# A hybrid decoder layer on one core: the value products move behind the next half's key products, and attention runs three blocks ahead instead of four

## The chip, the core and the metric

The kernel runs on one core of a Trainium2 chip. A core has five engines, each with its own instruction stream: TensorE (PE; its weight loads are shown as PEld), VectorE (DVE), ScalarE (ACT), GpSimd (POOL) and SyncE (SP, which issues most DMAs). They wait for each other through semaphores. The metric is the device time of one execution in microseconds; the figure to predict is the median of several runs.

## The reference, cut to what matters

One layer of a decoder: a normalised input is projected once, and the columns go to a gated short convolution, to sliding-window attention (8 query heads on 2 key heads, a learned sink per head) and to cross-attention of 4 heads into 256 memory tokens. The three outputs are gated, joined and projected.

```python
def _layer(...):
    h = _rmsnorm(x, g_pre)
    z = h @ w_in
    cb, cc, ch, cg, q, k, v, ag, mq, mg = _split_cols(z)
    ...
    out_a = jax.nn.silu(cg) * cb * conv
    ...
    o_b = _window_prompt(q, k, v, sink_g)          # banded, 128-query blocks
    out_b = jax.nn.silu(ag) * o_b
    o_c = _mem_attend(mq.reshape(n, t, MEM_HEADS, HEAD_DIM), mem_k, mem_v)
    out_c = jax.nn.silu(mg) * o_c
    y = jnp.concatenate([out_a, out_b, out_c], axis=-1) @ w_out
    return x + _rmsnorm(y, g_post), new_conv, new_k, new_v
```

The prompt has 4096 positions, and a sample part has 8 sequences of 8 new tokens with caches of their own. All is float32.

## The kernel before

The first 933 us are the input projection (seven products in place of eight on blocks of 520 positions, each product as three passes over a high and a low part). The change does not touch it. What follows is one loop over 32 output blocks of 128 positions, and a block for the sample tokens; in it the output projection and the attention of later blocks run through each other on TensorE.

**An output block** (class Block): its gated input, mix, is split into a high part (mh, ScalarE, line 1559) and a low part (ml, VectorE, line 1560; it reads mix and mh). Then 48 products y of 128x512 follow (line 1578): two halves p of the columns, eight steps k each, three passes a step. Ahead of a step (p, k), whatever stands in `starts` for it is called. So n = 16 b + 8 p + k counts the steps of all blocks, and an entry at (0, 4) or (1, 4) puts attention work between the y products there. Two PSUM banks (pool z) are for y.

**A half** h is the attention of one block of 128 queries: chunk c = h // 2 holds 256 positions, i = h % 2. It is done in two steps.

- first_half(h): `window_scores` (tiles ws, in two bank pairs w, of which there are two). Keys stand in a form in which each score is one product over all 128 rows and one over 64 rows (the low part of a key); two of the 64-row products lie side by side in the array, and are placed by `tile_position`. They run whole, half, half, whole. Then `memory_transposes` of the half before (xt, in bank pair x, of which there is one; two copies take it out, one on VectorE, the next on ScalarE, line 1345), and `window_probabilities`: ScalarE and VectorE mask, find the maximum, take exponentials (line 1265) and normalise (sm).
- second_half(h): `memory_scores` (xs, bank pair x, line 1332), for two heads of the chunk's 256 queries, then its maximum (xmx), exponentials (xp, line 1159) and the shares (xrd, line 1160), by which GpSimd multiplies xp (line 1168). `products` of the half before: the memory values (`both_values`, line 1057: column halves of 64, two at once), the window values over all keys (line 1218, column halves), and the quarters (line 1224: 64 rows by 64 columns, four at once). Where a new chunk begins, two transposes of its values (line 1643). Then `window_turns`: eight transposes of sm (wt, line 1353), which ScalarE copies out (wpt, line 1283), and from which GpSimd makes two masked tiles each (affine selects: wpv, line 1288, and wpt in place, line 1291). Last `gates`: VectorE multiplies the values into mix.

In the steady part, block b calls first_half(b + 4) at its step (0, 4) and second_half(b + 4) at (1, 4). The values of h - 1 belong to second_half(h). The first halves, 2 to 6, start by the table EARLY within blocks 0 to 2. The split of block b + 1 stands at the start of block b.

TensorE runs in the order in which the program records its work until block 26. The order on the other engines is chosen by a planner from what each instruction needs. GpSimd also issues the loads of keys (kst, line 1086) and queries (q, line 1099); its queue is in order like the others'. The sample tokens' attention is cut into stages (`sample_mem`, `sample_window`) that are called four times a block from block 26 on.

## Time and profile before

| | us |
|---|---|
| median of 3 runs (1539.02 to 1540.51) | 1540.0 |
| the profiled execution | 1536.39 |
| its span, first to last instruction | 1534.7 |
| first y product | 933.2 |
| a steady block (18 of them in 327.04 us) | 18.17 |
| first y product of block 25 | 1404.8 |

The profile comes from a single execution. It lists each engine's busy time, who ended an engine's wait, a chain of waits followed back from the last instruction, and timelines. An instruction's name such as `xt<-ident,xp` says which tile it writes and from which it reads. An entry of TensorE counts the passes: an ordinary float32 product stands twice, a transpose or a rounded float32 product once. A matmul's end is modelled, so the difference from one start to the next is its price, and not its own length.

### The profile page before, as it was taken

Reading aid. Unit: us, or ns where it says so; the run is one execution under the profiler, and the core shown is the slowest. Engines: PE = TensorE matmul, PEld = TensorE weight load, DVE = VectorE, ACT = ScalarE, POOL = GpSimd, SP = SyncE. Lnnn points to the kernel's source line nnn. Section 1 sums busy time; section 2 is a strip of 40 time slices with the busy share of each in tenths; the row PEclk is TensorE's granted clock in tenths of the full one; section 3 lists DMA queues with packets and bytes.
Section 4 is the critical chain, followed back from the end, with each engine's and each line's share of the span. In section 5 each row is a group of like instructions: output and inputs, shape, how many; then the busy total and the mean of one; then the engine's idle time right before and its main releaser. Section 6 shows DMA issues by size and latency. Waiting matters only on the chain.

```text
span 1534.7 us, 30061 instructions
## 1 busy us (share of the span) xinstructions
PE 1516.2 (99%) x11341; PEld 1387.8 (90%) x11341; DVE 1151.6 (75%) x1965; ACT 797.7 (52%) x1949; POOL 393.1 (26%) x635
## 2 busy tenths in 40 slices
PE   9999999999999999999999999999999999999998
PEld 9999999999999999999999998777888888887776
DVE  5779887899988777896776768776767677776643
ACT  6776665576322222444454547665555556655532
POOL 0223323211400000000100303644455454444310
PEclk9999999999999999999999999999999999999999
DMA  9989999978855333578776789977877778877432
GB/s 255 166 252 223 286 285 261 277 237 295 207 181 180 126 126 119 197 235 284 233 270 230 221 293 270 245 156 152 161 149 148 148 149 163 157 158 148 135 109 96
DMA packets 178453, 306.28 MB, mean 200 GB/s; under 512 B 34437, under 2 KB 108165, under 8 KB 178277
## 3 DMA queue, kind: packets, MB, share of 16 engines
q1 hardware_dynamic: 130901, 227.38, 48.4%
q0 software_dynamic: 46688, 75.93, 25.4%
q8 instruction: 90, 1.47, 0.4%
q10 hardware_dynamic: 720, 1.05, 0.2%
q14 instruction: 54, 0.44, 0.1%
HBM read 197.23 MB, written 108.05 MB: 199 GB/s over the span
## 4 chain that ended last, share of the span: by engine, by line
PE 68%; DMA 13%; DVE 9%; issue 5%; ACT 2%; POOL 1%; SPq 1%; ACTq 0%; DVEq 0%; POOLq 0%
PE c L368 33%; PE y L1578 21%; PE ws L1309 3%; PE wo L1057 2%; DMA place<-in_xt 2%; PE wt L1353 2%; PE xs L1332 2%; PE xt L1341 1%; PE wo L1218 1%; DMA nat<-in_x_p 1%; DVE z L375 1%; PE wo L1224 1%; DMA wr_3A<-in_w_in 1%; DMA zs<-qd 1%; DMA md<-th 1%
## 5 line engine op out<-in xcount | busy, mean ns | idle before, releaser
L1578 PE MATMUL y<-wo,mh 128*128 128x512 f32 (+1 forms) x1040 | 336.0, 393 | 0.0
L375 DVE TENSOR_TENSOR z<-c,z 128x520 f32<-128x520 f32 (+1 forms) x308 | 194.1, 644 | 80.8 <-PE c L368 79.4
L1578 PEld LDWEIGHTS y<-wo,mh 128*128 128x128 f32 x1040 | 194.4, 188 | 39.7 <-issue 2.0
L1578 PE MATMUL y<-wo,ml 128*128 128x512 f32 (+1 forms) x520 | 201.3, 387 | 0.0
L1578 PEld LDWEIGHTS y<-wo,ml 128*128 128x128 f32 x520 | 98.0, 188 | 17.5
L1168 POOL TENSOR_SCALAR xp<-xp,xrd 128x256 f32<-128x256 f32 x128 | 60.5, 481 | 197.4 <-DVE xrd L1160 197.3
L1265 ACT ACTIVATE sm<-sm,wnm 128x128 f32<-128x128 f32 x256 | 99.4, 389 | 14.2 <-DVE wnm L1259 11.6
L1159 ACT ACTIVATE xp<-xs,xnm 128x256 f32<-128x256 f32 x128 | 59.5, 470 | 89.6 <-DVE xnm L1157 86.9
L1585 DVE TENSOR_TENSOR yn<-y,gpost 128x512 f32<-128x512 f32 (+1 forms) x66 | 45.3, 686 | 62.6 <-PE y L1578 61.7
L1099 POOL DMA_DIRECT2D q<-qd x96 | 60.2, 635 | 116.9 <-DVE wo L186 56.7
L1319 DVE COPY_PREDICATED sm<-wmask,ws 128x512 f32<-128x512 uint8 x60 | 43.9, 735 | 49.3 <-ACT sm L1318 49.2
L1291 POOL TENSOR_SCALAR_AFFINE_SELECT wpt<-wpt 128x512 f32<-128x512 f32 x64 | 64.9, 1033 | 43.4 <-ACT wpt L1283 43.1
L737 POOL CAST wmask<-negs 128x256 uint8<-128x256 f32 x1 | 0.7, 686 | 266.3 <-DMA negs<-in_wmask 266.3
L1318 ACT COPY sm<-ws 128x512 f32<-128x512 f32 x60 | 35.1, 586 | 65.0 <-PE ws L1309 65.0
L1309 PEld LDWEIGHTS ws<-kst,q 128*128 128x128 f32 (+1 forms) x480 | 50.3, 187 | 12.0 <-PE y L1578 0.9
L1309 PE MATMUL ws<-kst,q 128*128 128x256 f32 (+1 forms) x480 | 59.5, 299 | 0.8 <-PE y L1578 0.5
L276 ACT ACTIVATE nat<-nat 104x1024 f32<-104x1024 f32 x40 | 42.3, 1058 | 26.0 <-DMA nat<-in_x_p 26.0
L407 ACT CAST zh<-z 128x520 fp32r<-128x520 f32 x56 | 33.3, 624 | 35.0 <-DVE z L375 31.9
L377 ACT COPY z<-c 128x520 f32<-128x520 f32 (+1 forms) x44 | 24.4, 554 | 49.6 <-PE c L368 46.5
L1086 POOL DMA_DIRECT2D kst<-qd x64 | 38.7, 617 | 42.9 <-issue 24.5
L1586 ACT ACTIVATE y<-y 128x512 f32<-128x512 f32 (+1 forms) x66 | 37.9, 575 | 21.5 <-DVE yn L1585 21.4
L1265 ACT ACTIVATION_READ_ACCUMULATOR sm<-sm,wnm 128x1 f32 x256 | 47.8, 187 | 0.0
(976 smaller groups left out, 5088.9 us busy)
## 6 DMA issues: line engine op xcount, KB each, us to landing
q<-qd POOLq DMA_DIRECT2D x96, 256.0 KB, 6.9
xr<-in_x_p SPq DMA_DIRECT2D x32, 512.0 KB
nat<-in_x_p SPq DMA_DIRECT2D x39, 416.0 KB
o_yp<-xr SPq DMA_DIRECT2D x31, 512.0 KB
md<-th POOLq DMA_DIRECT2D x48, 260.0 KB, 6.2
qd<-zh SPq DMA_DIRECT2D x48, 260.0 KB
qd<-z SPq DMA_DIRECT2D x48, 260.0 KB
kst<-qd POOLq DMA_DIRECT2D x60, 192.0 KB, 3.8
```

What stands on the lines that cost most here:

```text
L276: S.activation(t[:RG], t[:RG], AF.Square, accum_out=r[:RG, i : i + 1])
L368: TE.matmul(bank[:, :HW], l, r, start=first and i == 0, stop=last and i == 3 * KH - 1)
L375: add = lambda dst, other: V.tensor_tensor(dst, c, other, op=ALU.add)
L1099: G.dma_start(self.q[64 * half : 64 * half + 64, i : i + 4, :].rearrange("p (j v) n -> p j v n", v=2), heads(part, j, self.ts))
L1159: S.activation(p[:, i, :], s[:, i, :], AF.Exp, bias=nm[:, i : i + 1], scale=SCALE, accum_out=den[:, i : i + 1])
L1168: G.tensor_scalar(p[:, i, :], p[:, i, :], self.rds[h][:, i : i + 1], 0.5, op0=ALU.mult, op1=ALU.mult)
L1265: S.activation(sm[:, hh, :], sm[:, hh, :], AF.Exp, bias=nm[:, hh : hh + 1], scale=SCALE, accum_out=den[:, hh : hh + 1])
L1291: G.affine_select(p3, p3, pattern=[[0, 4], [1, P]], compare_op=ALU.is_ge, fill=0.0, base=0, channel_multiplier=-1)
L1309: TE.matmul(out(kvh, col, bank), q(kvh, col, bank)[r], k(kvh, part)[r], start=first, stop=True, skip_group_check=not first, **place)
L1319: V.copy_predicated(sm4, third["wmask"].unsqueeze(1).to_broadcast([P, 2, 2, P]), s4[:, :, :, 0:P])
L1578: TE.matmul(acc, self.hl[l][:, k], wo[k][c0 // 512][:, r, c0 % 512 : c0 % 512 + c1 - c0], start=j == 0, stop=j == passes * KT - 1)
L1585: V.tensor_tensor(yn[:m, c0:c1], acc[:m], gpost[:m, c0:c1], op=ALU.mult)
```

## The change

- `products` leaves second_half and goes to first_half, behind `window_scores`. `memory_transposes` of the half before now opens first_half, ahead of `window_scores`. second_half keeps `memory_scores` and `window_turns`.
- `window_scores` runs its whole-row products for both key heads first, then the 64-row ones. `products` runs the quarters first (in its own copy of the code of `band_values`), then the column halves over all rows, then the memory values. They are written to bank pair x, no longer to w.
- `memory_scores(i)` takes all four heads for the 128 queries of one block, instead of two heads for 256 queries. Maximum, exponentials and shares are three functions now, called for both pairs of heads in turn. The memory values are computed for two pairs of heads of 128 columns each.
- In the steady part, block b calls first_half(b + 3) at (0, 4) and second_half(b + 3) at (1, 4). The halves up to 7 start by the tables first_at and second_at, spread over blocks 0 to 4. The sample stages come three or four quarters later.
- `gates` follows `window_probabilities` in the steady part, and precedes it while the halves start early.

```diff
@@ cross_softmax, in three @@
-        def cross_softmax(self, h, s, now=True):
+        def cross_maximum(self, h, s):
...
+        def cross_exps(self, h, s, nm):
...
+        def cross_shares(self, h, p=None):
+            nb, den = CT // P, self.rds[h]
+            rd = self.rds[h] = tiny.tile([P, 4], F32, tag="rd", name=f"xrd{self.c}_{h}")
             V.reciprocal(rd[:, :nb], den[:, :nb])
...
@@ window_scores @@
-            for kvh, part in ((0, 0), (0, 1), (1, 1), (1, 0)):
+            for kvh, part in ((0, 0), (1, 0), (0, 1), (1, 1)):
...
-                    first = part == kvh and col == 0
+                    first = part == 0 and col == 0
...
         def memory_scores(self, i):
-            c, nb = self.c, CT // P
-            x = two_banks("x", f"xs{c}_{i}").rearrange("p h (b k) -> p h b k", b=nb)
-            for hh in range(2):
-                q = self.q[:, 2 * i + hh]
-                for n in range(nb):
-                    for part in range(2):
-                        TE.matmul(x[:, hh, n], q[:, n * P : n * P + P], third["mk"][:, part, 2 * i + hh, :], start=part == 0, stop=part == 1)
-            self.xps = [self.cross_softmax(2 * i + hh, x[:, hh]) for hh in range(2)]
+            c = self.c
+            x = two_banks("x", f"xs{c}_{i}").rearrange("p a (h k) -> p a h k", h=2)
+            for h in range(4):
+                q = self.q[:, h, i * P : i * P + P]
+                for part in range(2):
+                    TE.matmul(x[:, h // 2, h % 2], q, third["mk"][:, part, h, :], start=part == 0, stop=part == 1)
+            nms = [self.cross_maximum(2 * i + j, x[:, j]) for j in range(2)]
+            self.xps = [self.cross_exps(2 * i + j, x[:, j], nms[j]) for j in range(2)]
+            for j in range(2):
+                self.cross_shares(2 * i + j, self.xps[j])
 
         def memory_transposes(self, i):
-            c, self.pts = self.c, [[], []]
+            c, self.pts = self.c, []
             tx = two_banks("x", f"xt{c}_{i}")
-            for hh in range(2):
+            for j in range(2):
                 for kt in range(2):
-                    for n in range(CT // P):
-                        TE.transpose(tx[:, hh, kt * CT + n * P : kt * CT + n * P + P], self.xps[hh][:, n, kt * P : kt * P + P], ident)
-            for hh in range(2):
-                pt = work([P, 2, CT], "xpt", f"xpt{c}_{2 * i + hh}")
-                self.pts[hh] = [pt[:, kt] for kt in range(2)]
-                (S.copy if hh else V.tensor_copy)(pt, tx[:, hh].rearrange("p (a n) -> p a n", a=2))
+                    for hh in range(2):
+                        TE.transpose(tx[:, j, kt * CT + hh * P : kt * CT + hh * P + P], self.xps[j][:, hh, kt * P : kt * P + P], ident)
+            for j in range(2):
+                pt = work([P, 2, CT], "xpt", f"xpt{c}_{2 * i + j}")
+                self.pts.append(pt.rearrange("p a (h n) -> p a h n", h=2))
+                (S.copy if j else V.tensor_copy)(pt, tx[:, j].rearrange("p (a n) -> p a n", a=2))
 
         def window_turns(self, i):
             b = 2 * self.c + i
@@ -1355,18 +1366,31 @@
                 self.window_masks(b, kvh, tw[:, kvh], self.steps[kvh])
 
         def products(self, i):
-            c = self.c
-            banks = two_banks("w", f"wo{c}_{i}")
-            o = banks[:, 0, CT:]
-            both_values(o, *([(third["mkv"][:, kt, 256 + i * P : 256 + (i + 1) * P], self.pts[hh][kt]) for kt in range(2)]
-                             for hh in range(2)))
-            self.band_values(i, self.steps, banks[:, :, :CT], gated=False)
+
+            banks = two_banks("x", f"wo{self.c}_{i}")
+            o = banks[:, :, :CT].rearrange("p a (h q) -> p a h q", h=4)
+            for n in range(2):
+                for kvh in range(2):
+                    cs, rs = slice(64 * kvh, 64 * kvh + 64), slice(64 - 64 * n, 128 - 64 * n)
+                    v, p3 = self.steps[kvh][n]
+                    TE.matmul(o[cs, 1 - n], v[rs, cs], p3[rs, :, 64 - 64 * n : 128 - 64 * n], start=True, stop=False,
+                              tile_position=(64 - 64 * n, 64 * kvh))
+            for n in range(2):
+                for kvh in range(2):
+                    cs = slice(64 * kvh, 64 * kvh + 64)
+                    v, p3 = self.steps[kvh][n]
+                    TE.matmul(o[cs, n], v[:, cs], p3[:, :, 64 * n : 64 * n + 64], start=False, stop=True,
+                              tile_position=(0, 64 * kvh))
+            for j in range(2):
+                both_values(banks[:, 0, CT + j * P : CT + j * P + P],
+                            *([(third["mkv"][:, kt, 256 + j * P : 256 + (j + 1) * P], self.pts[j][:, kt, hh]) for kt in range(2)]
+                              for hh in range(2)))
             return banks
 
         def gates(self, i, banks):
             self.band_gate(i, banks[:, :, :CT].rearrange("p a (h q) -> p a h q", h=4))
-            gate = self.mix[:, 2 + i, :]
-            V.tensor_tensor(gate, gate, banks[:, 0, CT:], op=ALU.mult)
+            gate = self.mix[:, 2:4, i * P : i * P + P]
+            V.tensor_tensor(gate, gate, banks[:, 0, CT:].rearrange("p (j n) -> p j n", j=2), op=ALU.mult)
 
     def chunk_load(c):
         if c < NCH:
@@ -1615,70 +1639,64 @@
     def first_half(h):
 
         c, i = divmod(h, 2)
+        before = (chunks[(h - 1) // 2], (h - 1) % 2) if 2 < h <= 2 * NCH else None
+        if before:
+            before[0].memory_transposes(before[1])
         if c < NCH:
             chunks[c].window_scores(i)
-        if 2 < h <= 2 * NCH:
-            chunks[(h - 1) // 2].memory_transposes((h - 1) % 2)
+        banks = before[0].products(before[1]) if before else None
+        new_v = c < NCH and i == 0
+        if new_v:
+            chunks[c].values(chunks[c - 1].vts[2])
+            banks = two_banks("x", f"vtp{c}") if banks is None else banks
+            t = [banks[:, 1, CT + n * P : CT + n * P + P] for n in range(2)]
+            for n in range(2):
+                TE.transpose(t[n], chunks[c].vT[:, n * P : n * P + P], ident)
+        soon = first_at[h] > 16 * (h - 3) + 4
+        if before and soon:
+            before[0].gates(before[1], banks)
         if c < NCH:
             chunks[c].window_probabilities(i)
-            if i == 0:
-                chunks[c].values(chunks[c - 1].vts[2])
-                chunk_load(c + 1)
-            elif c + 1 < NCH:
-                chunks[c + 1].load_mix()
+        if before and not soon:
+            before[0].gates(before[1], banks)
+        if new_v:
+            for n in range(2):
+                S.mul(chunks[c].vts[1 + n], t[n], 0.5)
+            chunk_load(c + 1)
+        elif c + 1 < NCH:
+            chunks[c + 1].load_mix()
 
     def second_half(h):
 
         c, i = divmod(h, 2)
         if c < NCH:
             chunks[c].memory_scores(i)
-        banks = None
-        if 2 < h <= 2 * NCH:
-            banks = chunks[(h - 1) // 2].products((h - 1) % 2)
-        new_v = c < NCH and i == 0
-        if new_v:
-            banks = two_banks("w", f"vtp{c}") if banks is None else banks
-            t = [banks[:, 1, CT + n * P : CT + n * P + P] for n in range(2)]
-            for n in range(2):
-                TE.transpose(t[n], chunks[c].vT[:, n * P : n * P + P], ident)
-        if c < NCH:
             chunks[c].window_turns(i)
-        if 2 < h <= 2 * NCH:
-            chunks[(h - 1) // 2].gates((h - 1) % 2, banks)
-        if new_v:
-            for n in range(2):
-                S.mul(chunks[c].vts[1 + n], t[n], 0.5)
-
-
-    EARLY = {4: (first_half, 2), 15: (second_half, 2), 17: (first_half, 3), 22: (second_half, 3), 24: (first_half, 4),
-             28: (second_half, 4), 31: (first_half, 5), 37: (second_half, 5), 40: (first_half, 6)}
-
-    def starts_of(b):
-        steps = {n - 16 * b: (f_, h) for n, (f_, h) in EARLY.items() if n // 16 == b}
-        if b >= 2:
-            steps |= {4: (first_half, b + 4), 12: (second_half, b + 4)} if b > 2 else {12: (second_half, b + 4)}
-        return {(n // 8, n % 8): lambda f_=f_, h=h: f_(h) for n, (f_, h) in steps.items()}
+
+
+    first_at = {2: 4, 3: 21, 4: 35, 5: 47, 6: 59, 7: 71} | {h: 16 * (h - 3) + 4 for h in range(8, 2 * NCH + 1)}
+    second_at = {2: 14, 3: 27, 4: 40, 5: 52, 6: 64, 7: 76} | {h: first_at[h] + 8 for h in range(8, 2 * NCH + 1)}
+
+    def starts_of(i):
+
+        at = [(n, lambda h=h: first_half(h)) for h, n in first_at.items()] + [(n, lambda h=h: second_half(h)) for h, n in second_at.items()]
+        if i + 1 < len(blocks) and blocks[i + 1].b != 32:
+            at.append((max(16 * i, first_at.get(i + 2, 0) + 2), blocks[i + 1].split))
+        return {(p, k): lambda now=now: [fn() for fn in now] for p in range(2) for k in range(8)
+                if (now := [fn for n, fn in at if n == 16 * i + 8 * p + k])}
 
     def run(i, starts):
-        def split():
-            if i + 1 < len(blocks) and blocks[i + 1].b != 32:
-                blocks[i + 1].split()
-
-        if i != 1:
-            split()
         if i + 2 < len(blocks):
             blocks[i + 2].load()
         if blocks[i].b == 32:
             blocks[i].split()
-        if i == 1:
-            starts[1, 4] = lambda before=starts[1, 4]: (before(), split())
         left[0] = blocks[i].run(i == len(blocks) - 1, starts)
 
 
 
     stages = [sample_mem(0), sample_mem(1), sample_window()]
     sample_at = {}
-    for i, quarters in enumerate(((1, 3, 5, 7, 9), (8, 11, 13, 15, 16), (0, 8, 10, 12))):
+    for i, quarters in enumerate(((4, 7, 9, 11, 13), (12, 15, 16, 17, 19), (2, 12, 14, 16))):
         for n in quarters:
             sample_at.setdefault(n, []).append(stages[i])
     quarter = [0]
@@ -1696,11 +1714,13 @@
         if i == 26:
             turn.close()
         starts = starts_of(i)
-        run(i, starts | ({(p, k): late for p in range(2) for k in (1, 3)} if i >= 26 else {}))
+        for step in ((p, k) for p in range(2) for k in (1, 3)) if i >= 26 else ():
+            starts[step] = lambda before=starts.get(step, lambda: None): (before(), late())
+        run(i, starts)
     for stage in stages:
         for _ in stage:
             pass
-    run(31, {})
+    run(31, starts_of(31))
     run(32, {})
     finish_block()
     att.close()
```

More of the change, by code (lines that the diff above doesn't have):

```diff
@@ L1150, in cross_pair @@
             return *(self.cross_unit(2 * j + hh, pts[hh]) for hh in range(2)), both
[L1152 removed]
+        def cross_maximum(self, h, s):
+            c, nb = self.c, CT // P
+            mx, nm = (tiny.tile([P, 4], F32, tag=n, name=f"x{n}{c}_{h}") for n in ("mx", "nm"))
+            V.tensor_reduce(mx[:, :nb], s, axis=AX.X, op=ALU.max)
+            V.tensor_scalar(nm[:, :nb], mx[:, :nb], -SCALE, None, op0=ALU.mult)
+            return nm
+        def cross_exps(self, h, s, nm):
             c, nb = self.c, CT // P
             p = work([P, nb, 256], "p", f"xp{c}_{h}")
[L1155 to L1157 removed]
+            den = self.rds[h] = tiny.tile([P, 4], F32, tag="den", name=f"xden{c}_{h}")
             for i in range(nb):
                 S.activation(p[:, i, :], s[:, i, :], AF.Exp, bias=nm[:, i : i + 1], scale=SCALE, accum_out=den[:, i : i + 1])
+            return p
+        def cross_shares(self, h, p=None):
+            nb, den = CT // P, self.rds[h]
+            rd = self.rds[h] = tiny.tile([P, 4], F32, tag="rd", name=f"xrd{self.c}_{h}")
             V.reciprocal(rd[:, :nb], den[:, :nb])
[L1161 to L1162 removed]
+            if p is not None:
                 self.cross_factors(h, p)
[L1164 removed]
         def cross_factors(self, h, p):
```

9 lines of the change are left out of this document (2 added, 7 removed).

## The prediction

> **What bounds the kernel now.** I read the page's busy shares first, then TensorE's idle time by stage, then the chain of waits in order of time, then the timelines of VectorE, ScalarE and GpSimd around one block.
>
> ```profile
> span 1534.7 us, 30061 instructions
> PE 1516.2 (99%) x11341; PEld 1387.8 (90%) x11341; DVE 1151.6 (75%) x1965; ACT 797.7 (52%) x1949; POOL 393.1 (26%) x635
> ```
> ```profile
> core 0: us, PE busy (x) PEld busy (x) DVE busy (x) ACT busy (x) POOL busy (x), PEclk, DMA share, GB/s
> 1077.77:1404.81 327.04, 327.04 (x2035) 263.55 (x2034) 228.79 (x504) 190.51 (x667) 159.45 (x255) 1.00 0.79 156
> 933.20:1077.77 144.57, 140.75 (x893) 111.57 (x892) 106.52 (x247) 89.85 (x324) 74.04 (x125) 1.00 0.94 207
> 1404.81:1534.70 129.89, 121.99 (x742) 95.64 (x740) 70.98 (x157) 51.68 (x163) 26.96 (x56) 0.98 0.34 112
> ```
>
> The rows are stretches: the steady part (output blocks 7 to 24), the start (0 to 6), the tail. In the steady part TensorE is busy for all 327.04 us of 18 blocks, 18.17 us a block, at full granted clock. It never waits there, so only two things can change a block: what its own instructions take, and a wait that is put in. The start has 3.8 us of idle time, most of it for these:
>
> ```profile
> PE wt L1353 <- DVE sm L1273: 2.2, 2, 1.3
> PE wt L1353 <- DVE xrd L1160: 0.6, 2, 0.4
> PE ws L1309 <- PE y L1578: 0.5, 1, 0.5
> ```
>
> **What a change of array mode costs.** The chain of waits gives TensorE's time by group, each from the end of the one before it:
>
> ```profile
> 1101.39 5.46 PE y L1578 x24
> 1106.85 0.94 PE xs L1332 x8
> 1107.80 1.01 PE wo L1057 x8
> 1108.81 0.86 PE wo L1218 x8
> 1109.67 0.59 PE wo L1224 x8
> 1110.27 0.37 PE wo L1643 x2
> 1110.63 0.87 PE wt L1353 x8
> 1111.51 5.50 PE y L1578 x24
> 1117.00 1.81 PE ws L1309 x16
> 1118.81 0.87 PE xt L1341 x8
> ```
>
> L1057 and L1218 are the same work in the same mode (two 64-column halves side by side), but L1057 enters the mode: 1.01 against 0.86, so 0.15 us for entering it. The quarters (L1224) are half of that work, 0.43, and take 0.59: 0.16. Two transposes cost 2 x 0.109 = 0.22 (xt: 0.87 / 8) and take 0.37 behind the quarters: 0.15. In ws, eight whole and eight half-height products (these in pairs at once) are twelve steps of 0.118 (xs: 0.94 / 8), 1.42, and take 1.81: 0.39 for going into half height and out. Five changes a block: 0.85 us.
>
> **The change on TensorE.** The same products, transposes and moving columns are issued (the memory values go from 256 columns once to 128 columns twice, with as many passes), so the streaming time stays. Modes now run: whole, half height (end of ws), quarters, column halves, whole. That is 0.195 + u + 0.16 + 0.15. The step u, half height to quarters, stands nowhere in the trace; it lies between nothing (the row split stays) and the dearest change, 0.195. I take 0.17, the mean of the five, since the step is again a new mode. Saved: 0.85 - 0.505 - 0.17 = 0.175 us (0.15 to 0.345) for each of 30 product stages: 5.2 us (4.5 to 10.4). The Trainium skill (TensorEngine Tiling (Array Packing), Key Properties) says that changing the tiling mode drains TensorE, not just a change of tile; by that u is not nothing, and the sum would be the 5.2. Twice as many weight loads for the memory values cost between nothing and 8 x 0.01; I take nothing, as the column halves work side by side and half of L1218's step of 0.215 lies over each pair of loads.
>
> **The change around it: the factors come late.** Before, the step at (1,4) of a block (memory scores) was followed by values and turns, then 24 y products, then ws, and only then by xt, which needs the normalised probabilities xp. Now the values have left this step, and xt stands ahead of ws. From the first xs to the first xt was 0.94 + 2.83 + 0.87 + 5.50 + 1.81 = 11.9 us (2.83: the three wo groups and L1643); it is now 0.94 + 0.87 + 5.50 = 7.3, and 7.75 to the second pair of heads. What must fit into it:
>
> ```profile
> 1146.82 1.04 PE L1353 MATMUL wt<-ident,sm 128*128 128x128 f32 x8
> ```
> ```profile
> 1130.11 0.48 ACT L1159 ACTIVATE xp<-xs,xnm 128x256 f32<-128x256 f32 x1 [1.37 <-DVE xnm L1157]
> 1131.03 1.07 ACT L1283 COPY wpt<-wt 128x512 f32<-128x512 f32 x2
> 1132.13 1.05 ACT L1559 CAST mh<-mix 128x1024 fp32r<-128x1024 f32 x1
> ```
> ```profile
> 1131.16 0.17 DVE L1160 RECIPROCAL xrd<-xden 128x2 f32<-128x2 f32 x1 [0.26 <-ACT xp L1159]
> 1133.21 1.41 DVE L1560 TENSOR_TENSOR ml<-mix,mh 128x1024 fp32r<-128x1024 f32 x1 [0.16 <-ACT mh L1559]
> ```
> ```profile
> 1131.43 0.94 POOL L1168 TENSOR_SCALAR xp<-xp,xrd 128x256 f32<-128x256 f32 x2 [0.86 <-DVE xrd L1160]
> 1132.33 1.21 POOL L1288 TENSOR_SCALAR_AFFINE_SELECT wpv<-wpt 128x512 f32<-128x512 f32 x2
> 1133.51 2.20 POOL L1291 TENSOR_SCALAR_AFFINE_SELECT wpt<-wpt 128x512 f32<-128x512 f32 x2
> 1135.66 0.65 POOL L1099 DMA_DIRECT2D q<-qd  x1
> ```
>
> Two things are seen here. A select takes 0.6 us, but the pair that meets ml takes 2.20 instead of 1.21: 1.0 us more, until ml has ended. And GpSimd's order before is factors first, then selects. In the changed program ScalarE copies wpt before the exponentials, and GpSimd's order is, in turn, "four selects, four factors" in one block, and "wpv, q issue, two factors, wpt, wpv, two factors, wpt" in the next. Count from the first xs. wt is complete at 0.94 + 1.04 = 2.0. ScalarE has wpt at 2.7 and 3.1, the exponentials (0.92 a pair of heads, 1130.11 to 1131.03) at 4.0 and 4.9, then mh to 5.95, and VectorE starts ml at 6.0. The shares come 0.3 behind each exponential: 4.3 and 5.3.
> - Selects first: GpSimd starts at 2.75, selects 4 x 0.6 to 5.15, factors 4 x 0.46 to 7.0. With ml across them 8.0. Due at 7.75: TensorE waits 0.25 us.
> - Mixed order: wpv to 3.35, q issue to 4.0, factors from 4.35 to 5.25, wpt and wpv to 6.45, ml 1.0, factors to 8.35: a wait of 0.6 us.
>
> The mean is 0.43 us a block (nothing without ml's 1.0, 0.8 if the semaphores add 0.1 at each of four hand-overs). Behind the waiting xt stand ws, the values and all y products of the block, so the whole of TensorE moves by it.
>
> Other moves. The values now write bank pair x, of which there is one: they wait for the two copies of xt out of it. In order these are 0.68 on VectorE and, waiting for it, 0.59 on ScalarE, some 1.5 us with hand-overs:
>
> ```profile
> 1137.98 0.68 DVE L1345 COPY xpt<-xt 128x512 f32<-128x512 f32 x1
> 1138.69 0.59 ACT L1345 COPY xpt<-xt 128x512 f32<-128x512 f32 x1 [1.17 <-DVE xpt L1345]
> ```
>
> The cover is ws with its change of mode, 1.42 + 0.195 = 1.6: nothing, with 0.1 to spare; without the cover 1.5 a block. The gates must empty x before the next xs, 2.5 us of values and 5.5 of y later; VectorE has about 6 us of work there: nothing. Gates, copies, exponentials and loads keep their number and size; the q issue on GpSimd is counted above, and SyncE's mix loads have whole blocks of lead.
>
> **The sum.** Steady (blocks 5 to 27, 23 of them): 23 x (0.43 - 0.175) = +5.9. Seven more stages in start and tail: -1.2. The start spreads its steps: the waits of 3.3 us go, but scores and the next xt are 7 k-steps apart four times, 21 y products for 24, 0.7 us less cover: 4 x (0.43 + 0.68) = 4.4, so +1. In the tail the sample's steps move by three or four quarters with the attention and still end before block 30 does: 0. Together +5.7 us on 1536.4, the time of the profiled execution (span 1534.7): 1542.1. The runs shown have a median of 1540.0, 3.6 above that execution, so I predict 1546 us.
>
> **Rivals.**
> - *Factors in time: faster.* GpSimd keeps its turn and ml waits behind it. Seen once, in the tail:
>
> ```profile
> 1462.45 1.22 POOL L1291 TENSOR_SCALAR_AFFINE_SELECT wpt<-wpt 128x512 f32<-128x512 f32 x2
> 1463.00 1.75 DVE L1560 TENSOR_TENSOR ml<-mix,mh 128x1024 fp32r<-128x1024 f32 x1 [0.16 <-ACT mh L1559]
> ```
>
> Here the selects took 1.22 and ml 1.75. Then factors end at 7.0 and 7.35, ahead of 7.75; it decides from 7.75 down. Only the 5.2 us are left: 1535. Against it: in the steady rows ml wins. The Trainium skill (SBUF — State Buffer, Who interferes with whom) says that whichever of the two starts first holds the shared port for its whole instruction and the other fully blocks; the trace has both orders, and by that rule a start of ml some tenths of a us later would give this rival's time.
> - *Waits as large as the saving.* 0.17 us a block: 1540.
> - *The bank pair binds too.* If xt's copies start late behind ml, the spare 0.1 us is gone and each block waits some 0.4 us at wo in addition: 23 x 0.4 = 9, 1555.
> - *Not as said.* In the built program the values do stand right behind ws, quarters first, so I give this nothing.
>
> **How the numbers follow.** Forecast 0.42, in time 0.26, even 0.17, bank pair 0.15. About 0.2% (3 us) is what a measurement can tell from no change. Faster takes the first rival and 0.01 of the even case: 0.27. Same: 0.18, from the even case and the forecast's edge. Slower: 0.55. As both signs are likely, the forecast's own range is 1541 to 1551; the whole reaches to 1533 (u near nothing, no wait) and to 1558 (0.8 us of wait).
>
> **What would show it.** Right: xt waiting for POOL xp in nearly every steady block, some 0.2 us and 0.6 us in turn; xp pairs of 1.9 us across ml where 0.94 stood; ws to the last value with four changes, 0.175 less in all; periods near 18.4. Wrong: no wait at xt and periods near 18.0; wo waiting for ACT xpt; a step u well under 0.15; idle time in the start far from 5 us.

## The result, and the profile after

The changed kernel takes 1546.59 us (median of 9 runs, 1541.77 to 1551.16). The kernel before, run beside it, takes 1536.64 us (9 runs, 1534.44 to 1540.51). The ratio is 1.0059, with a 95% interval from 1.0040 to 1.0077: slower by 9 us (6 to 12). A second set of 9 runs of the same kernel, told below, gave 1.0052 (1.0036 to 1.0067), 8 us.

The time until the first y product varies from one execution to the next (930 us here, 933 us before), and the change does not touch what runs there. So the two profiled executions are compared from the first y product on, in three stretches: blocks 0 to 7, blocks 8 to 25, and the rest. Each row has the stretch, its length, then the busy time of TensorE, its weight loads, VectorE, ScalarE and GpSimd, and last TensorE's granted clock (1.00 is full), the busy share of the DMA engines and GB/s. Before:

```profile
933.21:1095.83 162.62, 158.80 (x1004) 126.08 (x1003) 119.10 (x275) 100.25 (x360) 83.86 (x141) 1.00 0.91 199
1095.83:1422.85 327.02, 327.02 (x2035) 263.55 (x2034) 228.80 (x504) 190.53 (x667) 156.06 (x250) 1.00 0.77 156
1422.85:1534.70 111.85, 103.95 (x630) 81.12 (x628) 58.38 (x129) 41.26 (x127) 20.54 (x45) 0.98 0.33 107
```

After:

```profile
930.96:1088.63 157.67, 152.51 (x1004) 122.75 (x1003) 108.33 (x251) 90.44 (x327) 75.07 (x125) 1.00 0.86 197
1088.64:1421.45 332.81, 330.69 (x2180) 268.84 (x2178) 218.01 (x505) 186.17 (x667) 159.63 (x255) 1.00 0.69 154
1421.45:1540.30 118.85, 111.73 (x726) 88.24 (x724) 65.46 (x153) 48.75 (x160) 28.59 (x56) 0.99 0.33 111
```

From the first y product to the end it is 601.5 us before and 609.3 after: +7.84. The 18 steady blocks give +5.79 of it, 18.49 us a block for 18.17. The other two stretches must be read together, since with three blocks ahead instead of four the attention of one block moves from the first to the last: -4.95 and +7.00, so +2.05.

TensorE's weight loads show the wait in the steady stretch (engine, what it waited for, us in total, times, the longest):

```profile
PEld xt L1352 <- POOL xp L1176: 8.2, 28, 0.6
```

And this is GpSimd there, in two blocks that follow each other, first the mixed order, then four selections and four factors (start, length of the whole group):

```profile
1216.28 0.64 POOL L1297 TENSOR_SCALAR_AFFINE_SELECT wpv<-wpt 128x512 f32<-128x512 f32 x1 [0.70 <-ACT wpt L1292]
1216.86 0.61 POOL L1099 DMA_DIRECT2D q<-qd  x1
1217.91 0.93 POOL L1176 TENSOR_SCALAR xp<-xp,xrd 128x256 f32<-128x256 f32 x2 [0.45 <-DVE xrd L1170]
1218.81 0.63 POOL L1300 TENSOR_SCALAR_AFFINE_SELECT wpt<-wpt 128x512 f32<-128x512 f32 x1
1219.40 0.62 POOL L1297 TENSOR_SCALAR_AFFINE_SELECT wpv<-wpt 128x512 f32<-128x512 f32 x1
1220.01 1.89 POOL L1176 TENSOR_SCALAR xp<-xp,xrd 128x256 f32<-128x256 f32 x2
...
1235.03 1.23 POOL L1297 TENSOR_SCALAR_AFFINE_SELECT wpv<-wpt 128x512 f32<-128x512 f32 x2 [9.53 <-ACT wpt L1292]
1236.20 1.22 POOL L1300 TENSOR_SCALAR_AFFINE_SELECT wpt<-wpt 128x512 f32<-128x512 f32 x2
1237.41 2.85 POOL L1176 TENSOR_SCALAR xp<-xp,xrd 128x256 f32<-128x256 f32 x4
```

VectorE's ml at the same places:

```profile
1219.49 1.61 DVE L1584 TENSOR_TENSOR ml<-mix,mh 128x1024 fp32r<-128x1024 f32 x1 [0.39 <-ACT mh L1583]
...
1238.25 1.23 DVE L1584 TENSOR_TENSOR ml<-mix,mh 128x1024 fp32r<-128x1024 f32 x1 [0.39 <-ACT mh L1583]
```

The weight loads of xt, which need those factors:

```profile
1221.50 0.14 PEld L1352 LDWEIGHTS xt<-ident,xp 128*128 128x128 f32 x1 [0.27 <-POOL xp L1176]
1221.95 0.31 PEld L1352 LDWEIGHTS xt<-ident,xp 128*128 128x128 f32 x3 [0.32 <-POOL xp L1176]
...
1240.32 0.31 PEld L1352 LDWEIGHTS xt<-ident,xp 128*128 128x128 f32 x3 [0.23 <-POOL xp L1176]
```

A pair of factors takes 0.93 us by itself. In the mixed order the pair that ml meets takes 1.89, and four factors take 2.85 with ml across them: 1.0 us late each time. The first ml took 1.61 instead of 1.23, since it came while a selection was still running. The Trainium skill (SBUF — State Buffer, Who interferes with whom) has this as a lock that the one who comes first keeps for its whole instruction; the trace shows both orders in these rows. In the mixed order the last factor is ready at 1221.90, and the last three transposes of xt load at 1221.95; with the selections first it is ready at 1240.26, and they load at 1240.32. From one block's first y product to the next it is 18.20 and 18.72 us in turn, where before it was 18.05 and 18.29.

### The profile page after: what moved, and what is told of

It is laid out like the page before. It is cut to its first block, busy times and chain, and to the rows that moved or that the text cites. A ratio compares the mean times of both kernels' runs of the same rounds, so it can differ in the third digit from the quotient of the medians.

```text
span 1540.3 us, 30416 instructions
## 1 busy us (share of the span) xinstructions
PE 1520.7 (99%) x11581; PEld 1397.0 (91%) x11581; DVE 1137.5 (74%) x1965; ACT 791.0 (51%) x1949; POOL 393.2 (26%) x635
## 4 chain that ended last, share of the span: by engine, by line
PE 76%; DMA 7%; DVE 5%; POOL 5%; ACT 4%; issue 3%; ACTq 0%; SPq 0%; DVEq 0%; POOLq 0%
PE c L368 47%; PE y L1602 15%; DMA nat<-in_x_p 3%; PE ws L1318 3%; POOL xp L1176 3%; PE wo L1382 2%; PE wo L1057 2%; PE xs L1340 1%; PE wt L1364 1%; PE xt L1352 1%; DMA md<-th 1%; PE wo L1376 1%; POOL wpt L1300 1%; ACT xp L1164 1%; DMA x_0B<-in_xt 1%
## 5 line engine op out<-in xcount | busy, mean ns | idle before, releaser
L1176 POOL TENSOR_SCALAR xp<-xp,xrd 128x256 f32<-128x256 f32 x128 | 84.9, 675 | 34.8 <-DVE xrd L1170 34.7
L1297 POOL TENSOR_SCALAR_AFFINE_SELECT wpv<-wpt 128x512 f32<-128x512 f32 x62 | 40.4, 665 | 145.4 <-ACT wpt L1292 145.3
L1328 DVE COPY_PREDICATED sm<-wmask,ws 128x512 f32<-128x512 uint8 x60 | 40.6, 732 | 38.2 <-ACT sm L1327 38.2
L1292 ACT COPY wpt<-wt 128x512 f32<-128x512 f32 x64 | 34.6, 589 | 64.2 <-PE wt L1364 64.2
L1155 DVE TENSOR_REDUCE xmx<-xs 128x2 f32<-128x512 f32 x64 | 41.5, 686 | 29.9 <-PE xs L1340 29.8
L1356 ACT COPY xpt<-xt 128x512 f32<-128x512 f32 x30 | 17.6, 586 | 87.3 <-DVE xpt L1356 87.3
L1318 PE MATMUL ws<-kst,q 128*128 128x256 f32 (+1 forms) x480 | 55.8, 298 | 0.0
L1300 POOL TENSOR_SCALAR_AFFINE_SELECT wpt<-wpt 128x512 f32<-128x512 f32 x64 | 42.1, 669 | 43.3 <-ACT wpt L1292 43.1
L1356 DVE COPY xpt<-xt 128x512 f32<-128x512 f32 x30 | 20.8, 692 | 42.5 <-PE xt L1352 42.4
```

The costliest lines, as they stand in the source:

```text
L1155: V.tensor_reduce(mx[:, :nb], s, axis=AX.X, op=ALU.max)
L1176: G.tensor_scalar(p[:, i, :], p[:, i, :], self.rds[h][:, i : i + 1], 0.5, op0=ALU.mult, op1=ALU.mult)
L1300: G.affine_select(p3, p3, pattern=[[0, 4], [1, P]], compare_op=ALU.is_ge, fill=0.0, base=0, channel_multiplier=-1)
L1318: TE.matmul(out(kvh, col, bank), q(kvh, col, bank)[r], k(kvh, part)[r], start=first, stop=True, skip_group_check=not first, **place)
```

## The experiments

Each measurement is set against runs of the kernel before on the same chip. A second profiled execution of the kernel before (expected and measured below) has the same steady blocks to 0.03 us and 601.4 us from the first y product on.

**The changed kernel again.**

> The changed kernel itself once more, for a second profiled execution. If the 4 us between the profiled execution (1542.05) and the median of its runs (1546.6) lie in the steady blocks, then this execution has more blocks above 18.2 and 18.7 us than the three seen; if in the stages ahead of the attention, then the first y product starts later than at 931 us.

Measured: 1542.39 us (9 runs), ratio 1.0052 as said above. Its stretches:

```profile
928.37:1087.43 159.06, 154.00 (x1004) 124.01 (x1003) 108.27 (x251) 90.46 (x327) 75.06 (x125) 0.99 0.84 195
1087.43:1420.29 332.86, 330.73 (x2180) 268.76 (x2179) 217.92 (x504) 186.16 (x667) 159.64 (x255) 1.00 0.68 154
1420.29:1539.20 118.91, 111.79 (x726) 88.22 (x724) 65.12 (x153) 48.76 (x160) 28.60 (x56) 0.98 0.33 111
```

Neither case. The steady blocks repeat to 0.05 us over 18 blocks, those that are longer than their neighbours among them, and the first product comes earlier, not later. What differs is the first stretch (159.06 for 157.67) and the time ahead of it. All of the difference in the first stretch lies in block 3 (25.04 us for 23.65), where TensorE's granted clock is at half for 3.4 us:

```profile
998.92:1002.32 3.40, 3.35 (x16) 2.89 (x17) 0.69 (x1) 0.58 (x1) 2.65 (x5) 0.50 0.92 230
```

So the 1.4 us say nothing about the change. Where the longer runs of the first set lost their 4 us, these two profiles do not show. The four longest (1547.28 to 1551.16 us) had a mean granted clock of 0.997, the profiled one 0.999, and 0.002 of 1540 us is an estimated 3 us; but in the second set the clock does not order the runs like that, so it stays open.

**The split moved away from the factors.**

```diff
-            at.append((max(16 * i, first_at.get(i + 2, 0) + 2), blocks[i + 1].split))
+            at.append((max(16 * i + (10 if 4 < i < 26 else 0), first_at.get(i + 2, 0) + 2), blocks[i + 1].split))
...
-            S.copy(hi, src)
-            V.tensor_tensor(lo, src, f(hi), op=ALU.subtract)
+            for x in (S.copy(hi, src), V.tensor_tensor(lo, src, f(hi), op=ALU.subtract)):
+                if 5 < b < 27:
+                    tc.keep_in_program_order(x)
```

> The changed kernel, but the split of the next block's mix (mh on ScalarE, ml on VectorE) is issued at step (1,2), pinned ahead of the memory scores' softmax, for blocks 6 to 26. Theory (the factors are late because ml holds the port that GpSimd needs, and because mh and ml stand between the scores and xt): the pairs of xp on GpSimd go back from 1.9 to 0.94 us in these blocks, TensorE no longer waits for xp at xt, the steady periods fall from 18.2 and 18.7 to about 18.0, and 21 blocks x 0.45 us = 9 us go: about 1537. Rival (the loss lies in the start and the tail, or in the products' new place, and the waits at xt only replace other waits): 1543 to 1547, with periods above 18.2. Rival (VectorE is the next to bind, the maxima of xs come some 0.6 us late behind ml): xt still waits, for an xp that is late by its exponentials, some 0.2 us a block: 1541.

Measured: 1534.43 us (10 runs), ratio 0.9996 (0.9979 to 1.0012), 8 us less than the changed kernel on the same chip. The steady stretch, and GpSimd's part of the block with the mixed order, the order being that of the changed kernel:

```profile
1085.80:1411.62 325.82, 325.69 (x2179) 268.68 (x2178) 220.67 (x504) 188.95 (x665) 142.16 (x255) 1.00 0.76 157
```
```profile
1212.75 0.93 POOL L1176 TENSOR_SCALAR xp<-xp,xrd 128x256 f32<-128x256 f32 x2 [0.91 <-DVE xrd L1170]
...
1214.85 0.92 POOL L1176 TENSOR_SCALAR xp<-xp,xrd 128x256 f32<-128x256 f32 x2
```

The shares come 0.46 us later than in the changed kernel ([0.91] for [0.45]), because the maxima of xs now stand behind ml, and still TensorE hardly waits for them (325.69 of 325.82 us are busy, and xt's weight loads wait for factors once, 0.3 us): both pairs take 0.93. It is 18.10 us a block for 18.49. GpSimd's busy time in the stretch falls from 159.63 to 142.16, 0.97 us a block. The theory is right, and since the order on GpSimd stayed, it is the place of the split (mh and ml) alone that did it. The loss in start and tail was not the whole, and VectorE, one rival, is later but not too late.

**One k-step more cover.** Cover is the work of TensorE between the scores and xt, under which the other engines must finish.

```diff
-... {h: first_at[h] + 8 for h in range(8, 2 * NCH + 1)}
+... {h: first_at[h] + 7 for h in range(8, 2 * NCH + 1)}
```

> The changed kernel with the second half of each steady stage one k-step earlier, at (1,3), so that three y products, 0.69 us, more lie between the memory scores and xt; the split stays where it is. Theory (the cover is too short by 0.2 and 0.7 us in turn): xp pairs still take 1.9 us across ml, but the waits at xt fall to nothing in one block and to 0.1 us at most in the other; periods about 18.0; about 1537. Rival (the x bank pair binds too): xs now waits for the gates and the copies of vt that empty the pair, what xt gains xs loses, some 0.3 us in every second block: 1541. Rival (the loss is elsewhere): 1546.

Measured: 1534.05 us (10 runs), ratio 0.9997 (0.9981 to 1.0012). TensorE's 324.66 us are all busy, 18.04 us a block, 17.95 and 18.12 in turn, so there is no wait at xt, and none at xs, and no weight load of theirs waits either:

```profile
1086.33:1410.99 324.66, 324.66 (x2179) 268.81 (x2178) 218.91 (x503) 188.29 (x667) 159.71 (x255) 1.00 0.72 158
```

The planner changed something with it: in every second block GpSimd now has its four factors together, ahead of three of the selections, so there this run does not separate cover from order. In the other blocks the order is still four selections, then four factors, in 2.80 us across ml, and the wait is gone as well: there it is the cover. As a kernel without waits the run gives the size of the two terms. Against it the changed kernel's blocks are 0.25 and 0.60 us longer (18.20 - 17.95, 18.72 - 18.12), which is the price of the late factors. Its own 18.04 against 18.17 before is what all the rest of the change saves, 0.13 us a block.

**One mode change put back.**

```diff
-            for kvh, part in ((0, 0), (1, 0), (0, 1), (1, 1)):
+            for kvh, part in ((0, 0), (0, 1), (1, 1), (1, 0)):
```

> The changed kernel with the window scores in the order of the kernel before (whole, half, half, whole height), so that the array goes out of half height once more ahead of the quarters: the one mode change that the change saved is put back and nothing else. Theory (a mode change costs 0.15 to 0.2 us of TensorE's time wherever it stands): ws takes 1.81 us for 1.62, the sum of the four groups grows by 0.17 to 0.2 us, about 30 blocks x 0.19 = 5.5 us: 1552. Rival (a change costs something only ahead of work whose operands are late): nothing, 1546.

Measured: 1548.53 us (4 runs), ratio 1.0095 (1.0066 to 1.0125), 6.1 us more than the changed kernel beside it. In the chain of waits (start, time from the end of the group before):

```profile
1244.38 1.81 PE ws L1318 x16
1246.19 0.59 PE wo L1376 x8
1246.79 1.01 PE wo L1382 x8
1247.80 0.87 PE wo L1057 x16
```

ws takes 1.81 for the 1.62 of the changed kernel, and the quarters 0.59 in both: going into quarters costs the same from half height as from the whole array, 0.16 by the prediction's working. The steady stretch grows by 3.44 us (336.30 for 332.86), 0.19 us a block. One change is worth what the prediction took for it.

**The values back where they were.** With them the edit puts back the order of the window scores, the bank pair w (neither is printed below) and the gates behind `window_turns`, and in the start it issues the split later. The four heads, the three blocks ahead and xt ahead of ws stay as changed.

```diff
@@ first_half @@
         if before:
             before[0].memory_transposes(before[1])
         if c < NCH:
             chunks[c].window_scores(i)
-        banks = before[0].products(before[1]) if before else None
...
@@ second_half @@
             chunks[c].memory_scores(i)
+        banks = before[0].products(before[1]) if before else None
...
             chunks[c].window_turns(i)
+        if before:
+            before[0].gates(before[1], banks)
```

> The changed kernel with its first part undone alone: the values go back behind the memory scores of the second half, into bank pair w, with the window scores in the order of before and the split behind the gates; the memory halves stay one block's four heads, the attention stays three blocks ahead, and xt stays ahead of ws. Theory (the loss comes with the values' new place, which takes 2.8 us of cover from xt): no wait at xt in the steady blocks, five mode changes as before, periods of 18.05 and 18.3 as before; against before only the start's and tail's part of the loss is left, 1 to 2 us: 1535 to 1537. Rival (three blocks ahead, or one block's four heads, cost by themselves): periods above 18.3 and 1540 or more.

Measured: 1535.43 us (10 runs), ratio 1.0007 (0.9982 to 1.0032). Its steady stretch has no wait:

```profile
1098.22:1426.06 327.84, 327.84 (x2179) 269.40 (x2178) 227.05 (x505) 186.84 (x667) 142.36 (x254) 1.00 0.71 156
```

18.21 us a block against 18.17. So one block's four heads, three blocks ahead, and xt ahead of ws cost 0.05 us a block together. The loss belongs to the values' new place and what follows from it: in this run GpSimd has its four factors ahead of the selections again, and ml comes behind them. The saving can be read here too. Against this run the one with more cover is 0.18 us a block shorter (18.21 - 18.04), neither waits, and TensorE's work differs by the values' place and the mode changes.

**More cover than needed.** The second half 6 k-steps behind the first, `first_at[h] + 6`.

> The changed kernel with the steady second half at (1,2), two k-steps earlier than in the changed kernel. Theory: xt needs no more than it got from one k-step, so nothing more is won there; the next to bind is what xs and wt wait for, the copies of vt out of bank pair x (they end 1.05 us ahead of xs in the profile of the changed kernel, and xs comes 1.38 us earlier) and the window's shares (1.1 us ahead of wt): 0.3 us a block, 6 us more than with one k-step, 1540. Rival (both have more room than the records show): 1534.

Measured: 1536.99 us (10 runs), ratio 1.0005 (0.9990 to 1.0019); 18.14 us a steady block, 0.10 more than with one k-step. The wait that was expected is there, and a third as large:

```profile
PEld xs L1340 <- ACT vt L1664: 2.0, 8, 0.3
```

Every second block, 0.25 us. wt, expected to wait for the shares, takes 0.94 for 0.87. The window for the second half is about one k-step wide: at 8 the factors bind, at 6 the bank pair.

**A thinner start.**

```diff
-    first_at = {2: 4, 3: 21, 4: 35, 5: 47, 6: 59, 7: 71} | {h: 16 * (h - 3) + 4 for h in range(8, 2 * NCH + 1)}
+    first_at = {2: 4, 3: 21} | {h: max(34 + 14 * (h - 4), 16 * (h - 3) + 4) for h in range(4, 2 * NCH + 1)}
...
+    second_at = {2: 14, 3: 27} | {h: first_at[h] + (6 if h < 11 else 7) for h in range(4, 2 * NCH + 1)}
```

> The changed kernel with the second half 7 k-steps behind the first (as in the run before, at (1,3) in the steady blocks) and with a start that is spread more thinly: the first halves of blocks 4 to 10 stand 14 k-steps apart instead of 12, the second halves 6 behind them, so that 8 k-steps lie between scores and xt where there were 7, and 6 between values and scores where there were 5. Theory (the start's waits, some 7 us of TensorE in the profile of the changed kernel, are xt waiting for its factors and xs waiting for the bank pair): most of them go, 3 to 4 us less than the run with the longer cover alone, 1530 to 1531, against 1534 of the kernel before. Rival (the work that the start no longer holds costs as much later): 1534.

Measured: 1532.52 us (12 runs), ratio 0.9978 (0.9963 to 0.9993). From the first y product on 598.1 us, 1.9 less than with the longer cover alone, half of what was expected. One new wait took the rest: the first row is TensorE's waits, the others VectorE.

```profile
PE wo L1376 <- ACT xpt L1356: 2.0, 1, 2.0
```
```profile
1072.39 1.70 DVE L1624 SCALAR_TENSOR_TENSOR xr<-yn,yst,xr 128x1024 f32<-128x1024 f32 x1 [1.07 <-POOL yst L1616]
1074.02 0.68 DVE L1356 COPY xpt<-xt 128x512 f32<-128x512 f32 x1
```

This is the prediction's third rival, in one place: the first half 10 stands at k-step 6, and VectorE's copy of xt stands behind the residual of the block before, which waits for a power (yst, part of the output's normalisation) that GpSimd does between its selections.

**Factors first on GpSimd**, as in the kernel before.

```diff
-            G.affine_select(p3, p3, pattern=[[0, 4], [1, P]], ...)
+            x = G.affine_select(p3, p3, pattern=[[0, 4], [1, P]], ...)
+            if b >= 8:
+                tc.keep_in_program_order(x)
```

(The other selection likewise.)

> The changed kernel with GpSimd's four selects pinned behind its four factors from block 8 on, as they stood in the kernel before; split and cover stay as changed. Theory (xt is late only because the factors stand behind selects and ml): the factors end 6.6 us after the first xs, ahead of xt at 7.3 and 7.75, the waits at xt are gone; but the selects are now those that meet ml and that xt no longer covers: they end some 10 us after xs, or 10.6 in the blocks with query loads between them, and the quarters ask for them at 10.2. So about 17.95 in one block, and up to 18.5 in the other, where TensorE waits for the selects at wo: 1536 to 1539. Rival (the selects have room too): 18.0 throughout, 1534. Rival (the order on GpSimd does not matter): 1542.

Measured: 1572.58 us (4 runs), ratio 1.023 (1.020 to 1.026); 19.85 us a steady block. The waits at xt are nearly gone, and the selections are what is late, by far more than expected:

```profile
PEld wo L1380 <- POOL wpt L1302: 18.1, 17, 1.6
```
```profile
1235.05 0.64 POOL L1099 DMA_DIRECT2D q<-qd  x1
1235.69 0.65 POOL L1302 TENSOR_SCALAR_AFFINE_SELECT wpt<-wpt 128x512 f32<-128x512 f32 x1
1236.29 0.64 POOL L1297 TENSOR_SCALAR_AFFINE_SELECT wpv<-wpt 128x512 f32<-128x512 f32 x1
1236.89 0.57 POOL L1620 TENSOR_TENSOR yst<-yst,mhalf 128x1 f32<-128x1 f32 x1
1237.42 0.64 POOL L1099 DMA_DIRECT2D q<-qd  x1
1238.06 0.65 POOL L1302 TENSOR_SCALAR_AFFINE_SELECT wpt<-wpt 128x512 f32<-128x512 f32 x1
```

The last selection, with a query load and the power ahead of it, starts at 1238.06 only, while the quarters of this block began behind ws at 1236.65 and the last two of them had to wait for it. The expectation had counted one load and left out the others and the power. Against the kernel without waits (18.04) a block is 1.8 us longer. About 1.0 are these waits, 0.3 come from three stretches of 3.41 us at half the granted clock (some 5 us in 18 blocks), and the rest is not shown. So the order on GpSimd is no free choice here: with the factors first, the selections and what the queue puts between them come too late for the quarters.

**The start, once more**, with no first half at k-step 6 of a block: `4: 34, 5: 48, 6: 62, 7: 76, 8: 89, 9: 103`, and 6 k-steps to their second halves.

> As the run with the longer cover and the thinner start, with two stages moved: the first halves of blocks 4 to 9 at steps 34, 48, 62, 76, 89 and 103, so that no first half stands at k-step 6 of a block, right behind the end of the block before on VectorE. There the values waited 2.0 us for the copies of xt out of bank pair x, since VectorE's first copy stood behind the residual of the block before, which itself waited for the power on GpSimd. Theory: this wait goes, nothing new comes, 2 us less than that run from the first y product to the end (598.1): 596, some 5 us less than before (601.4). Rival (VectorE is late there for other reasons): 598.

Measured: 1529.91 us (12 runs), ratio 0.9967 (0.9953 to 0.9982), 5 us less than before, and so faster than both kernels.

```profile
930.16:1084.18 154.02, 151.04 (x1005) 122.95 (x1004) 107.20 (x252) 90.97 (x329) 72.65 (x126) 1.00 0.89 201
1084.18:1408.83 324.65, 324.65 (x2180) 268.76 (x2178) 219.47 (x504) 188.32 (x667) 159.63 (x255) 1.00 0.71 158
1408.83:1527.30 118.47, 111.46 (x726) 88.76 (x724) 65.18 (x153) 48.68 (x158) 25.84 (x55) 0.98 0.33 111
```

597.1 us from the first y product on, against an expected 596: the wait of 2.0 us, wo for the copies of xt, has moved to the half at step 103, k-step 7 of its block, and is 1.2 there.

**The kernel before, again.**

> The kernel before once more, for a second profiled execution: its first y product started at 933.2 us in the first one, against 928.4 to 931.0 in five executions of the changed kernel and its variants. If that is chance, it starts anywhere between 928 and 933; if the change moves work ahead of the first product, again at 932 or later.

Measured: first y product at 932.15 us, 1535.23 us in one run. Still at the late end, as expected of a change that moves work there, but the changed kernel's variants reach 933.2 too (the run with the factors first), and the run with the values back began at 944.2 in its profiled execution, which took 1546.98 us while its median is 1535.43. In that execution two stretches of 3.41 and 6.83 us at half the granted clock lie ahead of the first product, by estimate 5 of the 11 us. The start varies by itself. Whether a small part of it belongs to the change stays open.

## Why the prediction was right, and where it was off

The direction, the cause and its place were right, and the time, 1546 against 1546.59, came out closer than the sum deserves: that is luck, since two errors cancelled.

- *The factors come late.* Right. Predicted waits of 0.25 and 0.6 us in turn; measured 0.25 and 0.60 against the same kernel with more cover. That ml decides it was shown by moving the split alone, and that the cover decides it by moving the second half, in those blocks in which the order on GpSimd stayed. Over the steady stretch it is 0.45 a block (18.49 - 18.04) for the predicted 0.43.
- *Why a little more than the turn of 0.25 and 0.60.* Two of the blocks (18.49 and 19.01 us) are some 0.3 us longer still, in both executions. The copy of wt is ScalarE's first step behind TensorE there; an ordinary block with the mixed order, and one of the two:

```profile
1178.42 1.07 ACT L1292 COPY wpt<-wt 128x512 f32<-128x512 f32 x2 [2.44 <-PE wt L1364]
```
```profile
1141.50 1.08 ACT L1292 COPY wpt<-wt 128x512 f32<-128x512 f32 x2 [2.72 <-PE wt L1364]
```

  ScalarE begins 0.28 us later, and all of it reaches TensorE, because nothing is left between the two. With one k-step more cover ScalarE is late at the same two places, and the blocks are as long as their neighbours.
- *The mode changes.* The mechanism and u were right (the quarters take 0.59, so 0.16 for the entry from half height where 0.17 was taken). The Trainium skill (TensorEngine Tiling (Array Packing), Key Properties), which the prediction cited for a drain at a change of tiling mode, agrees with that. The size was right too: 0.18 us a block against the run with the values back, for 0.175. Against the kernel before only 0.13 is left, since the rest of the change costs the 0.05 that the same run shows, and the prediction had put that at nothing. One term inside the saving was sized too small, the way back from column halves. Here is the chain of waits, of the kernel before in a block without transposes of a new chunk, and of the kernel without waits in such a block and in one with them:

```profile
1127.96 0.59 PE wo L1224 x8
1128.55 1.02 PE wt L1353 x8
```
```profile
1201.52 0.87 PE wo L1057 x16
1202.39 4.99 PE y L1602 x21
...
1219.48 0.87 PE wo L1057 x16
1220.35 0.37 PE wo L1654 x2
1220.72 4.80 PE y L1602 x21
```

  With no transposes behind the values it is y that leaves the column halves, and 21 products take 4.99 us for 4.80: 0.19. Before, wt came next and paid 0.15 (1.02 for 0.87). The prediction had taken 0.15 for both kinds of block.
- *The memory values in 128 columns.* Right: 0.87 us for 16 products; before, 0.86 for 8 once the entry into the mode is taken off. Nothing.
- *The bank pair and the gates.* Right in the steady blocks: no row has wo waiting for the copies of xt. In the start it is not nothing: there xs waits for the pair, see below.
- *The sum, its steady term.* 23 x (0.43 - 0.175) = +5.9, that is 4.6 for 18 blocks; measured 5.79. Of the 1.2 that are missing, 0.8 is the 0.05 a block just named, and 0.4 the waits of 0.45 for 0.43.
- *The sum, start and tail.* Predicted +1 in the start and -1.2 for seven other stages, -0.2 in all. Five of its steady blocks (5 to 7, 26 and 27) lie in the two outer stretches, so for these it comes to +1.1. Measured +2.05, and +3.5 in the second execution (159.06 + 118.91 - 162.62 - 111.85), of which 1.4 is the stretch at half clock: 1 us more in both. The idle time of TensorE in the start is as predicted, 5.2 us (157.67 - 152.51) for some 5. What the prediction did not have is that stages only 5 k-steps apart make xs wait until bank pair x is empty. In blocks 0 to 7 of the changed kernel TensorE's waits are

```profile
PE xt L1352 <- POOL xp L1176: 1.7, 2, 1.0
PE xs L1340 <- ACT vt L1664: 1.0, 2, 0.5
PE xt L1352 <- ACT xp L1164: 0.8, 1, 0.8
```

  and with 6 k-steps for 5, and 8 for 7 on the other side, the stretch is 2.8 us shorter (154.02 for 156.80 in the run with the cover alone). How the missing us divides between the waits for factors and those for the bank pair is not shown.
- *The base.* The prediction added 3.6 us, by which three runs lay above the profiled execution. Nine runs have a median of 1536.64, 0.25 from that execution: those three were high. So the change was predicted at +5.7, measured at 9 (6 to 12) and 8 (5.5 to 10); the base was 3.4 too high. From the first y product on the profile has 7.84 of the 9; the rest is the open part named at the repeated run.
- *The range.* Its ends do not follow from the prediction's own terms. Waits of 0.8 us give 23 x (0.8 - 0.175) - 0.2 = +14, some 1554 on its base of 1540, and not 1558; u at nothing and no wait give 1540 - 10.4, some 1530, and not 1533.

Of the rivals, "factors in time" fell with the waits, "waits as large as the saving" with their size (0.45 against 0.18), and "the bank pair binds too" with wo, which waits in no steady block; of the starts only the two thinner ones have that wait, once each. What stays open is what makes the time ahead of the first y product vary, and why ScalarE begins late at two fixed places.

## What to carry to other kernels

When work is moved away from between a producer and its consumer on the busiest engine, it was also cover: add up what the other engines must do in the time that is left, with each instruction's price where it meets its neighbour on a shared port, before counting what the move saves. Here moving the values saved 0.18 us of mode changes a block and brought waits of 0.45, and one k-step given back to the second half (0.69 us) kept the saving. And when a start is packed more tightly than the steady part, each of its waits has to be checked anew, the buffers' as well as the data's.

## What was not expected of the hardware

- The steady blocks repeat from execution to execution to some hundredths of a us, the two late starts of ScalarE (0.28 us) included, at the same blocks; the time ahead of the first y product varies by 5 us in nearly all executions (928.4 to 933.2). Small differences are best read from the first y product on, and with the granted clock beside them.
- In 5 of the 12 profiles TensorE's granted clock falls to half for 3.41 or 6.83 us somewhere ahead of the tail, at another place each time; one such stretch cost 1.4 us in the start of the changed kernel, and 1.6 to 1.9 in steady blocks of the run with the factors first.
- Leaving the column halves costs 0.15 us when transposes come next, and 0.19 when the wider y products do.
- One instruction of 1.23 us on VectorE made two factors of 0.93 us on GpSimd take 1.89, and where it came second it took 1.61 itself: one of the two is late by most of the other's length, whoever comes first.
